# The FFN input by seven block products: constants loaded later, tails stored by fours, another bank for the sums, another order of the steps

## The chip, the cores and the metric

The kernel runs on one core of a Trainium2 chip. Its engines work side by side, each through its own instructions in order: TensorE (PE in the profile; its weight loads are PEld), VectorE (DVE), ScalarE (ACT), GpSimd (POOL) and SyncE (SP, which only issues DMAs). The metric is the device time of one execution in microseconds (us). Lower is better.

## What is computed

One layer of a hybrid decoder for a prompt of 16 meta and 512 ordinary tokens and for 8 samples of 8 tokens, which share all weights. A mixing block (differential attention and a gated delta rule, merged by gates) is followed by an output projection and by a gated feed-forward network (FFN) with a short convolution. The change touches the FFN's input:

```python
xn = rmsnorm(x, p['ln_ffn_pre'])
up, gate = jnp.split(xn @ p['w_ffn_in'], 2, axis=-1)          # 1024 -> 2 x 2816
gate, new_ffn_conv = causal_dwconv(gate, ffn_conv_buf, p['ffn_conv_w'], p['ffn_conv_b'])   # width 3
x = x + rmsnorm((jax.nn.gelu(gate) * up) @ p['w_down'], p['ln_ffn_post'])
```

new_ffn_conv, the last two gate rows of the prompt and of each sample, is an output too; here these rows are called tails. The samples' convolution starts from rows that are given (state_ffn_conv).

## The kernel before

Matrix products are taken in three parts: each operand is split into a high part that TensorE takes exactly (`hi`, a cast on ACT, line 315) and the rest (`lo`, a subtraction on DVE, line 316), and hi x hi, hi x lo and lo x hi are added up (`mm`, line 273).

The stages, in order of time: the input projections; attention, with the paged cache of the samples; the recurrence of the delta rule (`main`) interleaved with a second stream (`rest`), which holds the samples' attention, then `ffn_consts`, then 16 gate products; the mixing; `out_proj`; `ffn_in`; `ffn_out`. `ffn_consts` loads the rows of the convolution's state, weights and bias with 18 small DMAs on ACT's queue, turns them with 22 transposes on PE and copies the result to `fw`, so that each channel's constants lie on its partition.

`ffn_in` works through 22 blocks of 128 channels, block m. The normalised input lies in four pieces of four 128-row slices each: `f["11"]` to `f["22"]`, the first digit for the half of the input channels, the second for the half of the tokens (290 columns). The first three blocks (`PLAIN`) are multiplied plainly (`plain_g` the gate half, `plain_u` the up half), while `differences` forms the sums of pieces t1 to t4 that the other blocks need. From block 3 on, gate and up of a block are one 2 x 2 product of blocks, made from seven products instead of eight, each of 12 matmuls. Per block, in the program's order before:

- `p1`: 11 x f11 into bank A, copied out by ACT (`saved`, line 1745); `p5`: s1 x t1 into bank C, copied out; `p2`: 12 x f21 into a bank "d", whose sum with the copy of p1 is the first half of the gate (`add_g`, lines 1751 to 1757, into `fpre`)
- `weights_g` and `load_u` of the next block: two raw tiles of gate weights (`wraw`, three buffers) and two of up weights (`raw`, three buffers), loaded by SP
- `p6`: s2 x t2 on top of A, copied out as u2; `p4` of the block before, on top of its A: the first up half, which DVE multiplies with the activated gate (`times`, lines 1810 and 1811), then `store`
- `weights_s` of the next block: s1 = a21 + a22 on POOL, s2 = s1 - a11 and s4 = a12 - s2 on DVE (`combine`, line 1711, tiles `sw`, three buffers), each then split (`divide`: `hw` on ACT, `lw` on DVE, seven and six buffers)
- `p3`: s4 x f22 on top of C, whose sum with u2 is the second half of the gate; `conv`: two copies of the tails on POOL (1792, 1793), the first tap on ACT (1797), two more taps on DVE (1799), the GELU on ACT (1802)
- `p7`: s3 x t3 on top of A; DVE adds the copy of p5 (1820), and POOL multiplies with the activated gate (`times` again)
- `weights_r` of the next block: s3 = a11 - a21 on POOL, and the splits of s3 and of a22 ("22"). s3 is the last reader of a21, the split of "22" that of a22; the buffers are then loaded again.

`begin` (line 1763) writes the samples' earlier rows from `fw` into `fpre`, on POOL, at the start of each block. `store` turns a block's 18 tail rows by a transpose into bank "s", copies them by ACT (1833) and sends them with two DMAs from POOL (1835, 1836). The eight banks of PSUM go by tags: two "d", three "t", one "s", and two that serve attention first and are "g" from the recurrence on; A is a "g" here and C a "t". The plain products, and the output projection, take their banks in turn (`psd`).

The text does not set the order of an engine's instructions by itself. A planner lays them out ahead of time: an instruction goes when its inputs and buffers are ready by the planner's own estimate, and among those that are ready the earlier one in the text goes first. Weights are so prepared a block or two ahead, and what the order really was is read from the trace.

## Time and profile before

| | |
|---|---|
| median of 3 runs | 1224.14 us (1222.51 to 1224.27) |
| the profiled execution | 1231.11 us |
| its span, from the first to the last instruction | 1229.4 us |
| mean granted clock of TensorE | 0.975 |
| block loop from block 3 to the last, about | 840 to 1075 us |
| plain blocks, about | 785 to 840 us |
| output projection, about | 740 to 785 us |
| 16 gate products beside the recurrence, from | 529 us |

How to read the lines below: a row of the timeline has the start in the span and the duration in us, the engine, the line of the kernel, the operation, the tile written and those read, the shape and the count; in brackets stands the idle time of the engine ahead of it and what ended that. A row of windows has the stretch, its length, and for each of PE, PEld, DVE, ACT and POOL the busy time with the number of instructions, then the granted clock, the DMA engines' busy share and GB/s. ACTq, POOLq and SPq are the sequencers of these engines, which issue DMAs. In the chain of waits each piece is what the piece after it waited for. The end of a matmul is modelled, and a wait for several things is put down to the one that came last.

### The profile page before, as it was taken

The numbers are of one execution on the slowest core, as the hardware profiler recorded it, in microseconds if no ns is written. First come the engines' busy times: TensorE is split into PE (matmuls) and PEld (weight loads), VectorE is DVE, ScalarE is ACT, GpSimd is POOL, SyncE is SP. The second block draws the span as 40 slices with busy tenths as digits, with TensorE's granted clock in tenths as the row PEclk, the third lists the DMA queues.
The fourth block names the chain that finished last, engine by engine and source line by source line (L and its number), as shares of the span: only waits on it lengthen the run. The fifth ranks groups of instructions, "written<-read, shape, count | busy, mean of one in ns | idle before, by whom it ended". The sixth has DMA issues, their size and how long they took to land. (4 is left out here: it accounts for less than half of the span.)

```text
span 1229.4 us, 23799 instructions
## 1 busy us (share of the span) xinstructions
PE 1151.9 (94%) x8699; PEld 1019.2 (83%) x8699; DVE 741.3 (60%) x1888; ACT 505.5 (41%) x1260; POOL 307.2 (25%) x427
## 2 busy tenths in 40 slices
PE   6999999979989989889999999969999999999996
PEld 5977797757677676589999987869999999999996
DVE  5456667585486487236235754598887878852224
ACT  5244445433343343233234434545554545643322
POOL 2122221141250231112010002473444444400000
PEclk9999999999999999789999999989999999999999
DMA  6274525737836946722322453303333323332222
GB/s 195 76 238 128 158 72 198 231 106 214 300 98 192 313 137 183 230 53 53 86 66 58 129 161 123 112 27 104 87 87 88 88 87 93 124 106 76 86 81 84
DMA packets 185204, 157.57 MB, mean 128 GB/s; under 512 B 13334, under 2 KB 147435, under 8 KB 185087
## 3 DMA queue, kind: packets, MB, share of 16 engines
q1 hardware_dynamic: 179569, 147.53, 39.4%
q0 software_dynamic: 4288, 5.16, 1.5%
q10 hardware_dynamic: 1230, 3.35, 0.9%
q8 instruction: 69, 1.13, 0.4%
q14 instruction: 48, 0.39, 0.1%
HBM read 146.12 MB, written 9.88 MB: 127 GB/s over the span
## 5 line engine op out<-in xcount | busy, mean ns | idle before, releaser
L316 DVE TENSOR_TENSOR wlo<-wraw,whi 128x512 fp32r<-128x512 f32 x196 | 148.6, 775 | 149.5 <-ACT whi L315 147.9
L273 PE MATMUL ps_d<-xhi,whi 128*128 128x256 f32 (+2 forms) x704 | 219.9, 313 | 0.0
L273 PE MATMUL ps_d<-xhi,wlo 128*128 128x256 f32 (+2 forms) x704 | 214.3, 305 | 1.2 <-DVE wlo L316 1.2
L273 PE MATMUL ps_d<-xlo,whi 128*128 128x256 f32 (+2 forms) x704 | 214.3, 304 | 0.3 <-DVE xlo L316 0.2
L315 ACT CAST whi<-wraw 128x512 fp32r<-128x512 f32 x198 | 116.9, 611 | 163.2 <-PE ps_d L273 86.4
L273 PEld LDWEIGHTS ps_d<-xhi,whi 128*128 128x128 f32 x704 | 135.0, 192 | 7.8 <-issue 4.2
L273 PEld LDWEIGHTS ps_d<-xlo,whi 128*128 128x128 f32 x704 | 134.9, 192 | 3.6 <-issue 2.5
L273 PEld LDWEIGHTS ps_d<-xhi,wlo 128*128 128x128 f32 x704 | 134.8, 192 | 2.5 <-DVE wlo L316 1.6
L421 PE MATMUL ps_t<-consts,page 128*128 128x128 f32 x512 | 73.0, 282 | 8.6 <-DVE KT L1405 7.5
L421 PEld LDWEIGHTS ps_t<-consts,page 128*128 128x128 f32 x512 | 57.4, 143 | 25.1 <-issue 10.9
L273 PE MATMUL ps_g<-fhit,hw 128*128 128x290 f32 x228 | 69.6, 305 | 4.5 <-ACT u L1745 3.4
L273 PE MATMUL ps_g<-flot,hw 128*128 128x290 f32 x228 | 68.1, 299 | 0.0
L273 PE MATMUL ps_g<-fhit,lw 128*128 128x290 f32 x228 | 67.8, 297 | 0.0
L1405 ACT COPY KT<-ps_t 128x512 f32<-128x512 f32 x64 | 37.4, 585 | 64.8 <-PE ps_t L421 62.2
L1405 DVE COPY KT<-ps_t 128x512 f32<-128x512 f32 x64 | 43.7, 685 | 18.9 <-PE ps_t L421 18.8
L316 DVE TENSOR_TENSOR lw<-sw,hw 128x512 fp32r<-128x512 f32 x76 | 54.0, 711 | 0.3 <-ACT fy L1802 0.2
L315 ACT CAST hw<-sw 128x512 fp32r<-128x512 f32 x76 | 46.6, 613 | 7.6 <-DVE sw L1711 5.0
L273 PEld LDWEIGHTS ps_g<-fhit,hw 128*128 128x128 f32 x228 | 43.4, 190 | 6.9 <-ACT u L1745 3.9
L1797 ACT ACTIVATE fy<-fpre,fw 128x592 f32<-128x592 f32 x22 | 19.5, 884 | 66.0 <-DVE fpre L1757 66.0
L273 PEld LDWEIGHTS ps_g<-flot,hw 128*128 128x128 f32 x228 | 43.7, 192 | 0.0
L273 PEld LDWEIGHTS ps_g<-fhit,lw 128*128 128x128 f32 x228 | 43.7, 191 | 0.0
L273 PE MATMUL ps_s<-KT,qb 128*32 128x256 f32 x512 | 38.4, 402 | 1.4 <-DVE KT L1405 1.1
(663 smaller groups left out, 3149.3 us busy)
## 6 DMA issues: line engine op xcount, KB each, us to landing
page<-in_cache_k SPq DMA_DIRECT2D x128, 256.0 KB
page<-in_cache_v SPq DMA_DIRECT2D x128, 256.0 KB
wraw<-in_w_in SPq DMA_DIRECT2D x88, 256.0 KB
wraw<-in_w_ffn_in SPq DMA_DIRECT2D x50, 256.0 KB
wraw<-in_w_down SPq DMA_DIRECT2D x40, 256.0 KB
raw<-in_w_ffn_in SPq DMA_DIRECT2D x38, 256.0 KB
wraw<-in_w_out SPq DMA_DIRECT2D x16, 256.0 KB
x<-in_x_prompt SPq DMA_DIRECT2D x4, 512.0 KB
```

The costliest lines, as they stand in the source:

```text
L273: self.nc.tensor.matmul(out, lhsT, rhs, **kw)
L315: self.nc.scalar.copy(hi, raw)
L316: (eng or self.nc.vector).tensor_tensor(out=lo, in0=raw, in1=hi.bitcast(F32), op=ALU.subtract)
L421: self.nc.tensor.transpose(out, in_, self.ident[:k, :k])
L1405: (nc.scalar.copy if j % 2 else nc.vector.tensor_copy)(kt[:, :, 128 * j : 128 * j + 128], tp)
L1797: nc.scalar.activation(y, pre[:, 0:n], AF.Identity, bias=fw[:, m, 19:20], scale=fw[:, m, 16:17])
```

## The change

- `ffn_consts` is no longer called in `rest`. `ffn_in` calls it. It loads wider rows with nine DMAs, into tiles that are later to hold t3 and t4, and that lie where weights of the output projection have lain; the transposes and the copy to `fw` are a function `turn`, called after block 1's first plain gate half.
- Tails are gathered for four blocks in one tile (`TAILS`) and stored together: one transpose, one copy, two DMAs for four blocks, six times in all. The plain blocks call no `store`; the loop calls it after `p4` of the block before, where something waits.
- A is a bank "t" (three), C a bank "g" (two).
- `p7` goes behind `p1` of the next block, and the split of "22" goes behind that `p7`, so `s3` comes directly after `conv` in the text.
- The copy of line 1763 moves from `begin` to `conv`, and some tiles and adds lose their last two columns.

```diff
@@ -240,7 +241,6 @@
                         with ExitStack() as s:
                             yield from self.sample_attention(self.pool(s, "sa", side="right"))
                         self.gates, self.gtpool = {}, self.pool(sm, "gates", side="right")
-                        self.ffn_consts()
                         for i in range(16):
                             yield from self.gate(i)
 
@@ -1657,20 +1657,26 @@
         part(4, r4)
 
 
-    def ffn_consts(self):
+    def ffn_consts(self, pool):
+
         nc, a = self.nc, self.a
-        self.fw = fw = self.t(self.gtpool, [128, NF, 20], "fw", bufs=1)
-        p = self.ps("t")[:, : NF * 20].rearrange("p (k c) -> p k c", k=NF)
-        for k0 in range(0, NF, 4):
-            n = min(4, NF - k0)
-            nat = self.t(self.gtpool, [128, NQ], "gt", bufs=18)[:, : 128 * n]
-            sl = slice(128 * k0, 128 * (k0 + n))
-            nc.scalar.dma_start(nat[:16], a["state_ffn_conv"][0].rearrange("b j c -> (b j) c")[:, sl])
-            nc.scalar.dma_start(nat[16:19], a["ffn_conv_w"][0][:, sl])
-            nc.scalar.dma_start(nat[19:20], a["ffn_conv_b"][:, sl])
-            for k in range(n):
-                self.transpose(p[:, k0 + k], nat[:20, 128 * k : 128 * k + 128])
-        nc.vector.tensor_copy(fw, p)
+        fw = self.t(pool, [128, NF, 20], "fw", bufs=1)
+        rows = []
+        for tag, k0, k1 in (("flot4", 0, 9), ("fhit4", 9, 18), ("flot3", 18, NF)):
+            t = self.t(self.ftpool, [128, 4 * NC], tag)[:, : 128 * (k1 - k0)]
+            sl = slice(128 * k0, 128 * k1)
+            nc.scalar.dma_start(t[:16], a["state_ffn_conv"][0].rearrange("b j c -> (b j) c")[:, sl])
+            nc.scalar.dma_start(t[16:19], a["ffn_conv_w"][0][:, sl])
+            nc.scalar.dma_start(t[19:20], a["ffn_conv_b"][:, sl])
+            rows += [t[:20, 128 * k : 128 * k + 128] for k in range(k1 - k0)]
+
+        def turn():
+            p = self.ps("t")[:, : NF * 20].rearrange("p (k c) -> p k c", k=NF)
+            for k in range(NF):
+                self.transpose(p[:, k], rows[k])
+            nc.vector.tensor_copy(fw, p)
+
+        return fw, turn
 
     def ffn_in(self, sf, gx):
 
@@ -1683,7 +1689,8 @@
             self.t(self.gtpool, [128, NQ], "gt", bufs=18) if m < 18 else None
             for m in range(NF)
         ]
-        fw, f = self.fw, self.f
+        f = self.f
+        fw, turn = self.ffn_consts(pool)
         for j in range(1, 5):
             f[f"t{j}"] = tuple(self.block_t(p, j) for p in ("hi", "lo"))
 
@@ -1729,7 +1736,6 @@
             (a11, a12), (a21, a22) = st["raw"], st["rawu"]
             combine(st, "s3", a11, a21, ALU.subtract)
             divide(st, "s3")
-            divide(st, "22", a22)
 
         def product(ps, wt, x, first):
             hi, lo = wt
@@ -1741,8 +1747,9 @@
                 self.mm(ps, lo[k], xhi[:, k], start=False, stop=k == 3, **kw)
 
         def saved(ps, tag):
-            t = self.t(pool, [128, NC], tag, bufs=2 if tag == "p5" else 1)
-            nc.scalar.copy(t, ps)
+            n = NC if tag == "p1" else NC - 2
+            t = self.t(pool, [128, n], tag, bufs=2 if tag == "p5" else 1)
+            nc.scalar.copy(t, ps[:, :n])
             return t
 
         def add_g(st, half, ps, t):
@@ -1757,14 +1764,11 @@
             nc.vector.tensor_tensor(out=sv[:, 4 * half : 4 * half + 4, 2:10], in0=ss(ps), in1=ss(t), op=ALU.add)
 
         def begin(st):
-            m = st["m"]
-            st["pre"] = pre = self.t(pool, [128, 514 + 80], "fpre", bufs=2)
-            sv = pre[:, 514:].rearrange("p (b j) -> p b j", b=NB)
-            nc.gpsimd.tensor_copy(sv[:, :, 0:2], fw[:, m, 0:16].rearrange("p (b j) -> p b j", b=NB))
+            st["pre"] = self.t(pool, [128, 514 + 80], "fpre", bufs=2)
 
         def p1(st):
             begin(st)
-            st["A"] = self.ps("g")[:, :NC]
+            st["A"] = self.ps("t")[:, :NC]
             product(st["A"], st["11"], f["11"], True)
             st["p1"] = saved(st["A"], "p1")
 
@@ -1777,7 +1781,7 @@
             product(st["C"], st["s4"], f["22"], False)
 
         def p5(st):
-            st["C"] = self.ps("t")[:, :NC]
+            st["C"] = self.ps("g")[:, :NC]
             product(st["C"], st["s1"], f["t1"], True)
             st["p5"] = saved(st["C"], "p5")
 
@@ -1788,19 +1792,24 @@
         def conv(st):
             m, pre = st["m"], st["pre"]
             sv = pre[:, 514:].rearrange("p (b j) -> p b j", b=NB)
-            tail = self.t(pool, [128, 18], "ftail", bufs=2)
+            nc.gpsimd.tensor_copy(sv[:, :, 0:2], fw[:, m, 0:16].rearrange("p (b j) -> p b j", b=NB))
+            i, n = m % TAILS, min(TAILS, NF - m + m % TAILS)
+            if i == 0:
+                self.tails = self.t(pool, [128, 18 * TAILS], "ftail", bufs=1)[:, : 18 * n]
+            tail = self.tails.rearrange("p (r m) -> p r m", m=n)[:, :, i]
             nc.gpsimd.tensor_copy(tail[:, 0:2], pre[:, 512:514])
             nc.gpsimd.tensor_copy(tail[:, 2:18].rearrange("p (b j) -> p b j", b=NB), sv[:, :, 8:10])
-            n = 592
-            y_ = self.t(pool, [128, 594], "fy", bufs=2)
-            y = y_[:, 0:n]
-            nc.scalar.activation(y, pre[:, 0:n], AF.Identity, bias=fw[:, m, 19:20], scale=fw[:, m, 16:17])
+            y_ = self.t(pool, [128, 592], "fy", bufs=2)
+            y = y_
+            nc.scalar.activation(y, pre[:, 0:592], AF.Identity, bias=fw[:, m, 19:20], scale=fw[:, m, 16:17])
             for j in (1, 2):
                 nc.vector.scalar_tensor_tensor(
-                    out=y, in0=pre[:, j : j + n], scalar=fw[:, m, 16 + j : 17 + j], in1=y, op0=ALU.mult, op1=ALU.add
+                    out=y, in0=pre[:, j : j + 592], scalar=fw[:, m, 16 + j : 17 + j], in1=y, op0=ALU.mult, op1=ALU.add
                 )
             nc.scalar.activation(y, y, AF.Gelu_apprx_tanh)
-            st["y"], st["tail"] = y_, tail
+            st["y"] = y_
+            if i == n - 1:
+                waiting.append((m - i, n, self.tails))
 
         def times(eng, st, half, u):
             if gfs[st["m"]] is None:
@@ -1810,30 +1819,36 @@
             eng.tensor_tensor(out=gf[:, sl], in0=y_[:, sl], in1=u[:, 0:256], op=ALU.mult)
             eng.tensor_tensor(
                 out=gf[:, 512 + 32 * half : 544 + 32 * half].rearrange("p (b t) -> p b t", b=4),
-                in0=_strided(y_, 514, 10, TS)[:, 4 * half : 4 * half + 4],
+                in0=y_[:, 512:592].rearrange("p (b j) -> p b j", j=10)[:, 4 * half : 4 * half + 4, 2:10],
                 in1=u[:, 256:288].rearrange("p (b t) -> p b t", b=4),
                 op=ALU.mult,
             )
 
         def p7(st):
             product(st["A"], st["s3"], f["t3"], False)
-            nc.vector.tensor_tensor(out=st["p5"], in0=st["A"], in1=st["p5"], op=ALU.add)
+            nc.vector.tensor_tensor(out=st["p5"], in0=st["A"][:, : NC - 2], in1=st["p5"], op=ALU.add)
             times(nc.gpsimd, st, 1, st["p5"])
 
         def p4(st):
             product(st["A"], st["22"], f["t4"], False)
             times(nc.vector, st, 0, st["A"])
-            store(st)
-
-        def store(st):
-            m = st["m"]
+
+        def store():
+
+            if not waiting:
+                return
+            m, n, tails = waiting.pop()
             tp = self.ps("s")
-            self.transpose(tp[:18, :128], st["tail"])
-            rows = self.t(pool, [18, 128], "ftailT", bufs=1)
-            nc.scalar.copy(rows, tp[:18, :128])
-            sl = slice(128 * m, 128 * m + 128)
-            nc.gpsimd.dma_start(o["new_ffn_conv_prompt"][0, 0, :, sl], rows[0:2])
-            nc.gpsimd.dma_start(o["new_ffn_conv_sample"][0, :, :, sl].rearrange("b j c -> (b j) c"), rows[2:18])
+            self.transpose(tp[: 18 * n, :128], tails)
+            rows = self.t(pool, [18 * TAILS, 128], "ftailT", bufs=1)
+            nc.scalar.copy(rows[: 18 * n], tp[: 18 * n, :128])
+            sl = slice(128 * m, 128 * (m + n))
+            nc.gpsimd.dma_start(
+                o["new_ffn_conv_prompt"][0, 0, :, sl].rearrange("r (m c) -> r m c", c=128), rows[0 : 2 * n]
+            )
+            nc.gpsimd.dma_start(
+                o["new_ffn_conv_sample"][0, :, :, sl].rearrange("b j (m c) -> (b j) m c", c=128), rows[2 * n : 18 * n]
+            )
 
         def plain(ps, w, half, n):
 
@@ -1879,12 +1894,12 @@
         def plain_end(st):
             for half in range(2):
                 times(nc.vector, st, half, st.pop(("u", half)))
-            store(st)
-
-        sts = [{"m": m} for m in range(PLAIN)]
+
+        sts, waiting = [{"m": m} for m in range(PLAIN)], []
         plain_g(sts[0], 0)
         plain_u(sts[0], 0)
         plain_g(sts[1], 0)
+        turn()
         plain_g(sts[0], 1)
         conv(sts[0])
         plain_u(sts[0], 1)
@@ -1911,6 +1926,9 @@
         for m in range(PLAIN, NF):
             st = nxt
             p1(st)
+            if last:
+                p7(last)
+            divide(st, "22", st["rawu"][1])
             p5(st)
             p2(st)
             if m + 1 < NF:
@@ -1919,21 +1937,23 @@
             p6(st)
             if last:
                 p4(last)
+            store()
             if m + 1 < NF:
                 weights_s(nxt)
             p3(st)
             add_g(st, 1, st["C"], st["u2"])
             conv(st)
-            p7(st)
             if m + 1 < NF:
                 weights_r(nxt)
             last = st
+        p7(last)
         self.gf, self.gx, self.ghi, self.glo, self.room = gfs, gx, [], [], []
         for p, j in (("hi", 1), ("lo", 1), ("hi", 2), ("lo", 2)):
             self.make_room(p, j)
         for m in range(7):
             self.divide_gf(m)
         p4(last)
+        store()
 
     def make_room(self, p, j):
```

More of the change, by code (lines that the diff above doesn't have):

```diff
@@ L143 @@
 PLAIN = 3
+TAILS = 4
 FINE = 8
```

## The prediction

> **What bounds the kernel now.** I read the busy table first, then windows by stage, then the chain of waits inside the stage that the change rewrites.
>
> ```profile
> PE 1151.9 (94%) x8699; PEld 1019.2 (83%) x8699; DVE 741.3 (60%) x1888; ACT 505.5 (41%) x1260; POOL 307.2 (25%) x427
> ```
>
> ```profile
> 871.27:1053.41 182.14, 178.27 (x1291) 173.44 (x1290) 149.25 (x287) 94.50 (x196) 90.63 (x136) 1.00 0.31 88
> 1053.41:1064.55 11.14, 11.14 (x84) 10.92 (x83) 8.80 (x18) 7.61 (x17) 4.62 (x9) 1.00 0.25 73
> ```
>
> 94% says that TensorE is nearly full over the whole span, but that is an average. The two windows (length, then busy time of PE, PEld, DVE, ACT, POOL) lie between equal points of the loop over the blocks, the two-column add of line 1755, which runs once a step. The first holds 15 steps: 182.14 / 15 = 12.14 us each. The second holds one step near the end, for which no more weights are prepared: 11.14 us with 84 matmuls (seven products of twelve), and PE never idle. I take 11.2 us as the step that PE alone would set, so these 15 steps lose 15 x 0.94 = 14 us to something else. What it is, the chain shows, here its longest pieces over one step (start, duration, what):
>
> ```profile
> 949.05 1.29 POOL sw L1711
> 950.40 0.57 issue
> 950.98 0.42 DVE fpre L1751
> 951.49 0.61 DVE lw L316
> 952.12 0.69 DVE sw L1711
> 952.82 0.75 DVE fy L1799
> 953.86 0.83 DVE fy L1799
> 954.83 0.50 POOL fpre L1763
> 955.49 0.99 POOL gt L1810
> 956.69 1.28 POOL sw L1711
> 957.99 2.88 DMA raw<-in_w_ffn_in
> 961.03 1.29 POOL sw L1711
> ```
>
> PE isn't in it. It is a ring: the sum s1 on POOL (949.05), s2 on DVE in the "issue" piece, behind it in DVE's queue the second gate half (950.98), one split, s4, and the two convolution taps (952.82, 953.86); then POOL's product with the second up half (955.49), then the difference s3 (956.69), last reader of a raw weight buffer; then the load into that buffer (957.99), and the s1 of a later block waits for that load (961.03). One turn is 961.03 - 949.05 = 11.98 us, and with an odd longer turn the 12.14. DVE and POOL stand in order behind the late s1; PE merely follows.
>
> **The change part by part.**
>
> *Constants out of the gates' stage.* ffn_consts leaves the stream that runs beside the recurrence. ACT's queue there, then PE's, then the window after it:
>
> ```profile
> 522.57 0.33 ACTq L1668 DMA_DIRECT2D gt<-in_state_ffn_conv  x1
> ...
> 528.34 0.26 ACTq L1670 DMA_DIRECT2D gt<-in_ffn_conv_b  x1
> ```
>
> ```profile
> 525.21 1.14 PE L421 MATMUL ps_t<-consts,gt 20*128 20x20 f32 x8
> ...
> 528.90 0.58 PE L421 MATMUL ps_t<-consts,gt 20*128 20x20 f32 x4 [0.52 <-DMA gt<-in_ffn_conv_b]
> 529.42 0.58 PE L273 MATMUL ps_d<-xhi,whi 128*128 128x256 f32 x1
> ```
>
> ```profile
> 540.00:560.00 20.00, 18.60 (x134) 17.23 (x134) 7.97 (x21) 10.66 (x35) 5.78 (x4) 1.00 0.22 54
> ```
>
> From 525.21 to 529.42 PE does these transposes and waits for their rows; a dense gate product follows at once. ACT is held by 18 issues from 522.57 to 528.60. Both go: 529.42 - 525.21 = 4.2 us. What follows is nearly full on PE (18.60 of 20 us), so most of it should stay. Bounds: 0, if the recurrence's own chain sets the stage's end, and 4.5, with the two last transposes that come later. I take **-4.2**, since ACT, which carries that chain too, is released as early.
>
> [...]
>
> *Constants at the end of the output projection.* Nine DMAs on ACT in place of 18: by the rows above (528.34 - 522.57) / 17 = 0.34 us each, 3.1 us of ACT's queue. ACT where their buffers come free:
>
> ```profile
> 779.82 0.46 ACT L412 ACTIVATE y<-y,or 128x192 f32<-128x192 f32 x1 [1.55 <-POOL or L385]
> 781.39 1.06 ACT L1593 ACTIVATE ojunk<-xr 128x1024 bf16<-128x1024 f32 x1 [1.11 <-POOL xr L416]
> ```
>
> ACT idles 2.66 us in front of these two, which hides most; without that cover 3.1 us would fall on the chain that ends the projection. I take **+0.5**. The 22 transposes, 0.14 us each by the row at 525.21, come back on PE just ahead of the stall shown next, at 0 (3 us without it). The copy of fw comes back on DVE, which is full there: **+0.6** for a copy of 440 columns by its neighbours of 0.4 to 0.7 us, up to 1.9 if it is stretched as the split at 828.54 below is.
>
> *The store leaves the plain blocks.* This looks like the largest gain of all. PE's row, two windows, and DVE:
>
> ```profile
> 819.96 0.37 PE L421 MATMUL ps_s<-consts,ftail 128*18 128x128 f32 x1 [10.64 <-POOL ftail L1793]
> ```
>
> ```profile
> 809.30:819.90 10.60, 0.02 (x1) 0.00 (x0) 9.99 (x12) 4.69 (x9) 7.57 (x8) 0.71 0.00 1
> 820.00:824.00 4.00, 4.00 (x18) 4.00 (x19) 3.91 (x7) 3.09 (x6) 2.52 (x3) 0.50 0.25 70
> ```
>
> ```profile
> 819.30 0.42 DVE L1810 TENSOR_TENSOR gt<-fy,ps_s 128x256 f32<-128x256 f32 x1 [0.49 <-ACT fy L1802]
> ...
> 828.54 1.89 DVE L316 TENSOR_TENSOR wlo<-wraw,whi 128x512 fp32r<-128x512 f32 x3
> ```
>
> PE stands for 10.64 us before the first tail's transpose: its bank ps_s still holds an up half, which DVE reads only at 819.30. That transpose goes. But DVE is busy for 9.99 of these 10.60 us, and waits there for ACT, not for PE. Without the stall PE ends block 1 some 10 us sooner and then waits for the low weights that DVE makes at 828.54. So the stall moves to about 820-829, and I take **0**. Bounds: -2.5, DVE's idle share (0.6 in 10.6) over the 45 us of the plain blocks, an estimate; and +2.0, since after the stall PE had clock 0.50 for 4 us, and a new stall that ends later is followed by the same. [...]
>
> *The seven-product loop.* Three edits meet the ring: the copy of line 1763 leaves its place ahead of POOL's product; p7 goes behind the next p1, so that its add (line 1820) is ready later; and s3 is written ahead of that product. DVE and POOL there:
>
> ```profile
> 953.49 0.45 DVE L1820 TENSOR_TENSOR p<-ps_g,p 128x290 f32<-128x290 f32 x1
> ...
> 954.60 0.68 DVE L316 TENSOR_TENSOR lw<-raw,hw 128x512 fp32r<-128x512 f32 x1
> 955.20 0.68 DVE L316 TENSOR_TENSOR lw<-sw,hw 128x512 fp32r<-128x512 f32 x1
> ```
>
> ```profile
> 955.49 0.99 POOL L1810 TENSOR_TENSOR gt<-fy,p 128x256 f32<-128x256 f32 x1 [0.16 <-ACT fy L1802]
> ```
>
> The copy costs the ring nothing: the product also waits for the GELU on ACT, which came 0.16 us later. The add does cost, because it stands between the two taps: 953.86 - 953.49 = 0.37 us. The order on an engine is laid out ahead of time by readiness; with p7 one product later the add should fall behind the second tap, and with a small bubble between dependent taps 0.3 us is won. For s3 its place in the text isn't all: it needs one of three sw buffers, and the one it gets is free when s1's low part has been split, 955.20 + 0.68 = 955.88. The product was ready at 955.49, ahead of that, so POOL most likely still takes it first. Thus 15 x 0.3 = **-4.5**. Bounds: 0 (order as it was) and -14 (ring shorter than PE's step).
>
> The third bank takes away PE's wait for the bank of sums:
>
> ```profile
> 953.26 0.19 PEld L273 LDWEIGHTS ps_g<-fhit,hw 128*128 128x128 f32 x1 [0.36 <-ACT p L1745]
> ...
> 960.25 0.19 PEld L273 LDWEIGHTS ps_g<-fhi,whi 128*128 128x128 f32 x1 [0.41 <-PE ps_g L273]
> ```
>
> These 0.77 us a step are where PE feels the ring. Taken away here they come back elsewhere while the ring is longer than PE's step: 0 by itself; it lets PE take what the ring gives. Of the stores 16 transposes, 16 copies and 32 issues go. They sit on engines with room, and only some six steps outside the 15 are PE's own: **-0.3**. The divide of a22 is put behind p7; it ran behind that add already (954.60): 0.
>
> *Sum:* -4.2 + 0.5 + 0.6 + 0 - 4.5 - 0.3 = -7.9 us. The profiled execution took 1231.1 us (span 1229.4), so its like would take 1223.2. The median of the runs shown, 1224.14, is 7 us lower; the same difference from it gives 1216.
>
> **The rivals.**
>
> (a) *PE-bound.* s3 gets ahead of the product. For it: s3 could have started at 955.88 instead of 956.69, which brings the ring to 11.98 - 0.81 = 11.17, no longer than PE's step, and the text now asks for s3 first. Against it: the product is ready first. The loop gives 14 instead of 4.5: 1216 - 9.5 = **1206.5**.
>
> (b) *The ring stays.* The add keeps its place between the taps. For it: p7 had ended long before its add ran in this trace. Then only the gates' stage pays: -7.9 + 4.5 = -3.4, **1220.7**.
>
> (c) *Slower: the raw buffers.* There are three. a22 is released by the low split of "22" (954.60), which now needs a buffer that p7 frees one product, 11.2 / 7 = 1.6 us, later. In this trace it ends at 955.28, and s3 at 957.97. If it slips by more than those 2.7 us, both loads of the next pair leave after s3, in SP's order, and the one that s1 waits for comes second. Price: between one issue, 0.34 us as on ACT, and one more transfer, 2.88 us; half way 1.6 us a step, 15 x 1.6 = 24 us in place of -4.5: 1216 + 4.5 + 24 = **1245**. Against it: a slip of 1.6 is what to expect.
>
> **How the numbers follow.** Forecast 0.43, (a) 0.28, (b) 0.17, (c) 0.07, and 0.05 for the upper ends together (nothing from the gates, +3.1, +1.9, +2.0). The forecast's own range is 1212 to 1221. To hold 8 in 10 the range takes in (a) with the plain blocks' -2.5, which is 1204, and (b) with part of its upper ends, 1224; outside lie (c), the last case and a little below, 0.17. A measurement of this kernel tells 0.2%, 2.4 us, from no change. Faster than 1221.7: the forecast, (a), and somewhat less than half of (b), 0.76; within: most of the rest of (b), 0.12; slower: 0.12.
>
> **What would show it.** Right: the dense gate product at about 525; DVE as busy as before over 800-845, with PE's stall turned into a wait for wlo; in the loop both taps side by side, the add behind them, and steps of 11.8. Steps of 11.3 with PE idle nowhere show (a), steps of 12.1 with the same chain (b), a load of raw that lands later against s3 (c). The forecast is wrong if POOL or DVE is ordered in the loop in a way that this trace doesn't show, or if the plain blocks aren't DVE's.

## Result and profile after

The changed kernel takes **1216.32 us** (median of 5 runs, 1212.26 to 1217.38) against 1224.27 us before (5 runs, 1222.51 to 1228.41): ratio 0.9924, interval 0.9899 to 0.995, so 6 to 12 us faster. The profiled execution took 1217.38 us (span 1215.6), 13.7 less than the profiled execution of before.

Where the time went is best seen when the same instruction is looked up in the traces of several kernels, and the time from one such landmark to the next is compared. Five of the kernels are experiments of the next section: "consts" is before with the constants' part of the change alone, "tails" with the tails by fours alone, "order" with the order of the steps and the banks alone, "tails+order" is after with the constants in their old place, and "consts+tails" is after with the old order and the old banks. The landmarks are an ACT copy `pT` near 500 us, one of the key norms (ACT `gjunk`, at 540.30 in after and 553.50 in before), a DVE `y` of the output projection's last tiles near 765, the third and the eighteenth low split `lw<-raw` (15 steps of the loop apart; so the row of the plain blocks has the end of the projection and the first steps of the loop in it), an ACT copy `yT` near 1180, and DVE's last `yroot`. Times in us, each a difference of two starts in the timeline of one profiled execution:

```
                     before  tails  order  tails+order  consts  consts+tails  after
gates' stage          53.43  47.37  48.85        49.23   39.72         39.32  39.62
gates to projection  224.72 224.55 222.27       222.41  224.49        223.29 224.71
plain blocks          91.23  91.82  91.39        91.77   90.30         90.56  88.51
15 steps of the loop 182.42 182.17 186.57       184.49  182.06        182.28 180.95
FFN output           145.43 145.56 145.16       145.57  145.47        145.62 145.29
last products         25.20  25.76  25.66        28.14   25.33         25.75  28.53
```

Read the first row first. Wherever the constants are loaded in the gates' stage it takes 47 to 49 us (53 in before's profiled execution), wherever they are not, 39.3 to 39.7. No other row moves by more than 4.2 from before's value. The busy table hardly shows it:

```profile
PE 1143.0 (94%) x8683; PEld 1013.7 (83%) x8683; DVE 748.4 (62%) x1888; ACT 502.8 (41%) x1244; POOL 299.4 (25%) x395
```

94% again. The windows of the stage show it, first of before, then of after (length, busy time of PE, PEld, DVE, ACT, POOL, granted clock, DMA share, GB/s):

```profile
500.00:510.00 10.00, 8.17 (x51) 4.78 (x51) 2.12 (x7) 2.01 (x8) 3.34 (x3) 0.66 0.88 278
...
520.00:530.00 10.00, 6.98 (x47) 5.95 (x44) 3.10 (x13) 2.62 (x11) 1.19 (x2) 0.68 0.37 103
```

```profile
500.00:510.00 10.00, 8.51 (x64) 4.58 (x66) 3.62 (x10) 2.23 (x9) 3.89 (x3) 1.00 0.91 305
...
520.00:530.00 10.00, 10.00 (x76) 9.43 (x74) 2.96 (x10) 2.15 (x6) 1.54 (x2) 1.00 0.03 8
```

The granted clock was 0.68 in the ten microseconds around the constants and is 1.00 now, and PE is busy for all of them. The 0.66 at 500 to 510 is another matter: no other kernel with the constants in that place shows it (1.00 in each), so it belongs to that one execution of before: 53.4 against 48.5, some 5 of the 7 us by which it lay above its median.

The loop, in the chain of waits of after (start, duration, what), one turn:

```profile
932.32 1.30 POOL sw L1718
...
936.10 0.76 DVE fy L1806
...
937.63 0.45 DVE p L1829
938.08 1.20 DVE lw L316 x2
939.28 0.67 POOL gt L1820
939.94 0.02 issue
939.96 1.32 POOL sw L1718
941.27 0.02 issue
941.29 2.96 DMA raw<-in_w_ffn_in
944.25 0.02 issue
944.27 0.04 POOLq L1718
944.32 0.09 issue
944.41 1.29 POOL sw L1718
```

It is the ring of before, with the same members, and a turn of 944.41 - 932.32 = 12.09 us. PE's waits at the start and in the middle of the plain blocks, two rows of PE's timeline:

```profile
785.44 0.40 PE L273 MATMUL ps_t<-fhi,hw 128*128 128x290 f32 x1 [2.01 <-ACT hw L315]
...
811.59 0.58 PE L273 MATMUL ps_s<-fhi,whi 128*128 128x290 f32 x1 [4.60 <-ACT fhit L315]
```

4.60 us in place of 10.64, and 2.01 that are new.

### The profile page after: what moved, and what is told of

Same layout as the page of the kernel before. It is cut to its first block, busy times and chain, and to the rows that moved or that the text cites. A ratio compares the mean times of both kernels' runs of the same rounds, so it can differ in the third digit from the quotient of the medians.

```text
span 1215.6 us, 23653 instructions
## 1 busy us (share of the span) xinstructions
PE 1143.0 (94%) x8683; PEld 1013.7 (83%) x8683; DVE 748.4 (62%) x1888; ACT 502.8 (41%) x1244; POOL 299.4 (25%) x395
## 4 chain that ended last, share of the span: by engine, by line
PE 52%; DVE 17%; issue 15%; DMA 6%; POOL 5%; ACT 3%; SPq 0%; ACTq 0%; DVEq 0%; POOLq 0%
PE ps_d L273 22%; PE ps_g L273 9%; PE ps_t L273 8%; PE ps_s L273 6%; PE ps_t L421 6%; DMA raw<-in_w_ffn_in 2%; POOL sw L1718 2%; DVE lw L316 2%; DVE cy L651 1%; DMA page<-in_cache_v 1%; PE ps_m L273 1%; DVE KT L1405 1%; DVE fy L1806 1%; DVE gt L316 1%; DVE sw L1718 1%
## 5 line engine op out<-in xcount | busy, mean ns | idle before, releaser
L273 PE MATMUL ps_t<-fhit,hw 128*128 128x290 f32 x228 | 70.7, 310 | 3.7 <-DVE p L1829 3.1
L273 PE MATMUL ps_t<-flot,hw 128*128 128x290 f32 x228 | 67.6, 296 | 0.0
L273 PE MATMUL ps_t<-fhit,lw 128*128 128x290 f32 x228 | 67.5, 296 | 0.0
L316 DVE TENSOR_TENSOR lw<-sw,hw 128x512 fp32r<-128x512 f32 x76 | 62.4, 821 | 0.3 <-ACT hw L315 0.2
L273 PEld LDWEIGHTS ps_t<-fhit,hw 128*128 128x128 f32 x228 | 42.9, 188 | 9.4 <-DVE p L1829 6.4
L273 PEld LDWEIGHTS ps_t<-flot,hw 128*128 128x128 f32 x228 | 43.3, 190 | 0.0
L273 PEld LDWEIGHTS ps_t<-fhit,lw 128*128 128x128 f32 x228 | 43.1, 189 | 0.0
```

The costliest lines, as they stand in the source:

```text
L273: self.nc.tensor.matmul(out, lhsT, rhs, **kw)
L316: (eng or self.nc.vector).tensor_tensor(out=lo, in0=raw, in1=hi.bitcast(F32), op=ALU.subtract)
```

## The experiments

### One part of the change at a time

**The constants alone.** `ffn_consts` and `turn` as in the change, the copy of the samples' earlier rows moved to `conv`, the rest as before.

```diff
-                        self.ffn_consts()
...
-        fw, f = self.fw, self.f
+        f = self.f
+        fw, turn = self.ffn_consts(pool)
...
         plain_g(sts[1], 0)
+        turn()
```

> Before, with the constants' part of the change alone (nine loads at the end of the output projection, the turn after block 1's first plain gate half, the copy of the samples' earlier rows moved to conv). Theory 1, most of the gain is the gates' stage (4.2 us of PE) less what the end of the projection gives back: 3 to 6 us faster than before, so 1218 to 1221, with the first dense gate product at about 519 to 525 us in place of 529. Theory 2, the gain comes from the loop and the order of its steps: within 2 us of before. In both the 10.64 us wait of PE ahead of the first tail's transpose is still there.

Measured: 1215.12 us, ratio 0.9914 (0.9897 to 0.9932). That is 11 us, more than either theory gave it, and no less than the whole change. The wait ahead of the first tail's transpose, in PE's timeline, is still there and 1.9 us shorter:

```profile
812.15 0.37 PE L420 MATMUL ps_s<-consts,ftail 128*18 128x128 f32 x1 [8.73 <-DVE gt L1817]
```

**The tails alone.** `store` by fours, called once a step, none in the plain blocks; `saved` and `p7`'s add two columns narrower for room.

```diff
             times(nc.vector, st, 0, st["A"])
-            store(st)
...
                 p4(last)
+            store()
```

> Before, with the storing of tails by fours alone (and the narrower copies that make room for it). Theory 1: the 10.64 us wait of PE in the plain blocks goes, a shorter one comes later, and 1 to 4 us are won over the plain blocks, so 1220 to 1223; the loop keeps its 12.1 us a step. The prediction's own term says 0 here and 0.3 for the stores that are gone. Theory 2: within 1 us of before.

Measured: 1227.52 us, ratio 1.0008 (0.9999 to 1.0017): nothing that can be told, as in theory 2. PE's rows show what became of the 10.64 us:

```profile
815.38 0.58 PE L274 MATMUL ps_s<-fhi,whi 128*128 128x290 f32 x1 [6.16 <-DVE gt L1818]
...
824.65 0.61 PE L274 MATMUL ps_s<-fhi,wlo 128*128 128x290 f32 x1 [4.95 <-DVE wlo L317]
```

6.16 + 4.95 = 11.11 us of waits, the second of them for `wlo` where the prediction had put it. Taking away one of PE's waits moved it and did not shorten it.

**Order and banks alone.**

```diff
-            st["A"] = self.ps("g")[:, :NC]
+            st["A"] = self.ps("t")[:, :NC]
...
-            st["C"] = self.ps("t")[:, :NC]
+            st["C"] = self.ps("g")[:, :NC]
...
             p1(st)
+            if last:
+                p7(last)
+            divide(st, "22", st["rawu"][1])
             p5(st)
...
             conv(st)
-            p7(st)
```

> Before, with the order of the steps and the banks alone: A is a bank t and C a bank g, p7 stands behind the next block's p1, and the split of 22 behind that p7. Theory 1, the ring still sets the step: 12.1 us a step and a time within 1.5 us of before. Theory 2, and the prediction's own term: the add of line 1820 falls behind both taps and the step is 11.8 us, 4 to 5 us faster than before.

Measured: 1230.78 us, ratio 1.004 (1.0027 to 1.0052): 5 us slower, against both theories. The loss is in the loop (186.57 in the table). Two loads of its chain of waits:

```profile
929.98 3.09 DMA raw<-in_w_ffn_in
...
942.15 4.04 DMA raw<-in_w_ffn_in
```

The work between is the same in each step; some loads last 1 us longer.

**All but the constants**, that is after with the constants in their old place.

> After, with the constants loaded in the gates' stage as before (so tails by fours, the order of the steps and the banks are there). Theory 1: 1 to 4 us faster than before and 3 to 6 us slower than after, so 1220 to 1223; PE has the transposes at about 525 us again. If the granted clock is again below 0.8 at 500 to 530 us, that dip belongs to the constants' place there; if it is 1.00, the dip was that one execution's. Theory 2: nearly all of the 8 us stay, 1217.

Measured: 1230.64 us, ratio 1.0042 (1.0028 to 1.0055): 14 us slower than after, beyond both theories. The clock from 520 to 530 is 0.54. It is low (0.54 to 0.68) in before, tails, order and tails+order, and 1.00 in after, in consts alone and in consts with tails. The dip belongs to the constants' place.

**Constants and tails**, that is after with the old order and the old banks.

> After, with the old order of the steps and the old banks (so the constants' part and the tails by fours alone). Theory 1, order and banks are worth nothing by themselves because the ring sets the loop: within 2 us of after, 1214 to 1218, 12.1 us a step. Theory 2, they win here the 2 us that after's trace has in the loop over that of the constants alone: 1218 to 1219. Theory 3, they cost what they cost with the constants in the old place (5 us): 1211 to 1213.

Measured: 1214.76 us, ratio 0.9906 (0.9891 to 0.9921). After's interval and this one overlap: order and banks win nothing that can be told. Theory 1 holds.

### What in the gates' stage costs

Constants in their old place, the 18 DMAs too, but the transposes, now a function that `ffn_consts` returns, behind the third gate product.

```diff
-                        self.ffn_consts()
+                        turn = self.ffn_consts()
                         for i in range(16):
                             yield from self.gate(i)
+                            if i == 2:
+                                turn()
```

> Before, with the constants' 18 DMAs issued on ACT where they were, but their 22 transposes placed after the third gate product instead of ahead of the first. Theory 1, what the constants cost in the gates' stage is PE standing for their rows and the low clock (0.5 to 0.7 at 520 to 530 us) that follows: PE starts the dense product at about 519 us at clock 1.00, and 5 to 9 us are won, 1217 to 1221. Theory 2, it is ACT, held by 18 issues from about 517 to 523 us, that delays the recurrence and the products' copies: the first dense product may start early, but the stage ends no sooner and the time is within 2 us of before, 1224 to 1228.

Measured: 1229.64 us, ratio 1.0019 (1.0007 to 1.0032). Nothing is won; it is 2 us slower. Its timeline, ACT first and then PE, and its window:

```profile
516.58 0.27 ACT L901 COPY gv<-ps_g 128x128 f32<-128x128 f32 x1 [0.41 <-PE ps_g L275]
516.74 0.33 ACTq L1670 DMA_DIRECT2D gt<-in_state_ffn_conv  x1
...
523.61 0.26 ACTq L1672 DMA_DIRECT2D gt<-in_ffn_conv_b  x1
523.92 0.75 ACT L1504 ACTIVATE gt<-ps_d 128x256 f32<-128x256 f32 x2 [7.07 <-DMA gt<-in_ffn_conv_w]
...
524.36 0.58 PE L275 MATMUL ps_d<-xhi,whi 128*128 128x256 f32 x1 [5.22 <-ACT gt L1504]
```

```profile
516.00:518.00 2.00, 0.94 (x6) 0.78 (x7) 0.62 (x5) 0.43 (x3) 0.58 (x1) 1.00 0.69 191
518.00:520.00 2.00, 0.97 (x7) 0.63 (x5) 0.63 (x5) 0.00 (x0) 0.61 (x1) 0.85 0.92 243
520.00:522.00 2.00, 0.00 (x0) 0.00 (x0) 0.00 (x0) 0.00 (x0) 0.00 (x0) 0.50 0.25 66
...
526.00:528.00 2.00, 2.00 (x12) 2.00 (x11) 1.26 (x6) 0.27 (x1) 0.71 (x1) 0.50 0.00 0
528.00:530.00 2.00, 2.00 (x12) 2.00 (x12) 0.42 (x2) 0.00 (x0) 0.00 (x0) 0.59 0.00 0
```

No transpose stands in front of the dense product now, and it starts no sooner. PE idles 5.22 us for ACT's copy out of a bank "d", and that copy stands in ACT's queue behind the 18 issues: the last of them ends at 523.61 + 0.26 = 523.87, the copy starts at 523.92. (Issues don't count as busy, so the row calls the 7.07 us idle and names a DMA.) In after the same copy stands directly behind the same `gv`, from ACT's timeline:

```profile
517.38 0.27 ACT L899 COPY gv<-ps_g 128x128 f32<-128x128 f32 x1 [0.41 <-PE ps_g L273]
517.55 0.72 ACT L1502 ACTIVATE gt<-ps_d 128x256 f32<-128x256 f32 x2
```

PE's clock falls to 0.50 at about 519.4 (0.85 is the mean of the slice) and stays there until about 529.6, for 5 us of dense work. Theory 2 holds in its cause, ACT. But the dense product, which that theory let start early, didn't, and the time is 1.6 us above its range.

Then the same with the 18 DMAs issued by SP in place of ACT (`nc.scalar` to `nc.sync` in three lines), and nothing else changed.

> As the kernel with the transposes after the third gate product, but the 18 DMAs are issued by SP, not by ACT; nothing else differs. Theory, formed after that run: what costs is ACT's queue, in which 18 issues (516.74 to 523.87 us) stand ahead of the copies that free the banks of the first dense products; PE idles 5.2 us for them and then runs at clock 0.5 until about 529. Then ACT is free at about 517 here, the dense products start at about 519 at clock 1.00, and 6 to 9 us are won against before: 1218 to 1221. If the loads' mere presence, their landing or the transposes cost it, the time stays at 1226 to 1230. If SP's weight loads now stand behind the 18 issues, PE waits for weights a little later and part of the gain is lost, 1221 to 1225.

Measured: 1232.86 us, ratio 1.0056 (1.004 to 1.0072), 3 to 5 us slower still: the theory's number failed. In its timeline:

```profile
533.21 0.69 ACT L1504 ACTIVATE gt<-ps_d 128x256 f32<-128x256 f32 x2
...
534.51 0.56 PE L275 MATMUL ps_d<-xhi,whi 128*128 128x256 f32 x1
```

ACT was free, but the order laid out for it now has the recurrence's activations first and this copy at 533.21, 9 us later than with ACT issuing. So the edit did not do what it was to do. It speaks for the copy all the same. The start of ACT's copy and of the dense product in the kernels so far:

```
                         ACT's copy   dense product
before                       528.65          529.42
tails                        524.96          525.59
order                        525.00          525.76
tails+order                  523.68          524.53
transposes later             523.92          524.36
the same, DMAs on SP         533.21          534.51
consts                       517.14          518.67
consts+tails                 515.86          517.40
after                        517.55          519.08
```

The product follows the copy by 0.4 to 1.5 us in all nine, with the transposes in front of it or not. In the last three it doesn't wait for the copy: it follows the recurrence's matmuls.

### What sets the loop

If the ring of the raw loads sets the step, something that opens it must shorten the step. In after, s3 needs one of the three sw buffers. The first edit writes s3 over a11, which has no later reader.

```diff
-            combine(st, "s3", a11, a21, ALU.subtract)
+            nc.gpsimd.tensor_tensor(out=a11, in0=a11, in1=a21, op=ALU.subtract)
+            st["rs3"] = a11
```

> After, with s3 = a11 - a21 written over a11, so that it needs none of the three sw buffers and needn't wait for the split of s1's low part. Theory 1, the ring (load of raw, s1, s2, split of s1, s3, load of raw) sets the step and this wait is part of it: s3 starts 2 to 4 us earlier after s1, the loads of raw land before POOL asks for them, and the step falls from 12.1 to between 11.2 and 11.6 us, 8 to 14 us faster than after: 1202 to 1208. Theory 2, DVE's order or another buffer sets the step: 12 us still, within 2 us of after. Theory 3: a11's buffer comes free later and the wraw loads take over, slower than after.

Measured: 1217.59 us, ratio 0.9933 (0.9919 to 0.9946), the same as after. The edit did act. In the timeline (DVE, then POOL's s1, s3 and next s1, then SP's two loads of raw) s3 starts 2.4 us after s1 began, where it was 7.6:

```profile
940.90 0.68 DVE L316 TENSOR_TENSOR lw<-raw,hw 128x512 fp32r<-128x512 f32 x1
...
932.54 1.57 POOL L1718 TENSOR_TENSOR sw<-raw,raw 128x512 f32<-128x512 f32 x1 [1.63 <-DMA raw<-in_w_ffn_in]
934.97 1.28 POOL L1737 TENSOR_TENSOR wraw<-wraw,raw 128x512 f32<-128x512 f32 x1 [0.86 <-DVE sw L1718]
...
944.78 1.41 POOL L1718 TENSOR_TENSOR sw<-raw,raw 128x512 f32<-128x512 f32 x1 [1.79 <-DMA raw<-in_w_ffn_in]
...
936.28 0.37 SPq L1710 DMA_DIRECT2D raw<-in_w_ffn_in  x1
...
941.67 0.37 SPq L1710 DMA_DIRECT2D raw<-in_w_ffn_in  x1
```

But s1 needs both raw buffers. The load into the second leaves at 941.67, right behind the low split of "22" on DVE (940.90), s1 still waits 1.79 us for it, and a turn is 944.78 - 932.54 = 12.24 us. The ring closes over the other raw buffer. In the chain of waits most pieces are PE's now, with ACT's copy of p1 between them, for which PE waits about 0.5 us a step; whether that or the second buffer sets the 12.1 us that are left, this run doesn't tell.

The same edit on the constants' part alone, with the old order and banks:

> Before with the constants' part alone, and s3 written over a11. Theory 1, as with the edit on after: 8 to 14 us faster than 1215 (1201 to 1207) if the ring alone sets the step whatever the order of the steps; if the changed order and the third bank are what lets PE take a shorter ring, this one gains clearly less than the edit on after, 3 to 6 us. Theory 2: within 2 us of 1215.

Measured: 1222.42 us, ratio 0.9963 (0.995 to 0.9977), 6 to 7 us slower than without the edit, and against both theories. The loss isn't in the loop, of which 15 steps take 182.15 us (182.06 without the edit): by the landmarks of the first table it is in the row of the plain blocks, 95.75 against 90.30.

A fourth sw buffer, paid for with an lw buffer:

```diff
-            t = self.t(w7, [128, 4, 128], "sw", bufs=3)
+            t = self.t(w7, [128, 4, 128], "sw", bufs=4)
...
-            hi, lo = (self.t(w7, [128, 4, 128], tag, F32R, bufs=n) for tag, n in (("hw", 7), ("lw", 6)))
+            hi, lo = (self.t(w7, [128, 4, 128], tag, F32R, bufs=n) for tag, n in (("hw", 7), ("lw", 5)))
```

> After, with a fourth sw buffer, and one lw buffer fewer to make room. Theory 1: s3 no longer waits for the split of s1's low part, as with s3 in place; the step falls below 11.8 us, 4 to 14 us faster than after, unless the fifth lw buffer is missed. Theory 2: the wait for the buffer was not what held s3, within 2 us of after or slower by the missing lw buffer.

Measured: 1221.18 us, ratio 0.9961 (0.9946 to 0.9975), 5 us slower than after. s3 does start sooner, 5.8 us after s1 in the mean of the same 15 steps in place of 7.6, and these take 187.21 us all the same. The run can't say which of the two buffers did it.

Both raw buffers at once: s3 over a11 and s4 over a12, two sw buffers, and the memory of the third as a fourth raw buffer.

```diff
-            combine(st, "s4", a12, st["rs2"], ALU.subtract, nc.vector)
+            nc.vector.tensor_tensor(out=a12, in0=a12, in1=st["rs2"], op=ALU.subtract)
+            st["rs4"] = a12
...
-                t = self.t(w7, [128, 4, 128], "raw", bufs=3)
+                t = self.t(w7, [128, 4, 128], "raw", bufs=4)
```

> After, with a fourth raw buffer in the memory of the third sw buffer, which isn't needed when s3 is written over a11 and s4 over a12. Theory 1, the ring through the raw loads sets the step (in after the buffer that s3 releases, with s3 in place the one that the low split of 22 releases at 8.76 us of a 12.1 us step): with a fourth buffer both loads land before POOL asks for them, and the step is what PE needs, 11.3 us, plus its waits for banks of 0.2 to 0.6: 6 to 12 us faster than after, 1204 to 1210. Theory 2, the order on DVE and ACT (the tap behind s2 and s4, p1's copy behind the tap) sets 12.1 us whatever the buffers: within 3 us of after. Theory 3: the wraw buffers, now held until the splits of s3 and s4, take over, slower than after.

Measured: 1235.57 us, ratio 1.0079 (1.006 to 1.0097), 19 us slower than after: theory 3. Two rows of its waits from 870 to 1040 us, some 13 steps (total us, times, longest):

```profile
ACT whi L315 <- DMA wraw<-in_w_ffn_in: 23.1, 13, 2.2
...
PEld ps_t L273 <- DVE p L1831: 21.4, 14, 1.9
```

No wait for a raw load is left among them. The gate weights' load has taken its place, since their buffers are now held until the splits of s3 and s4 are done, and PE waits for the add behind it. With the old order and banks:

> The constants' part and the tails by fours with the old order and the old banks, and the fourth raw buffer. Theory 1: as with the edit on after, if the ring is all that lies above PE's step: 1204 to 1210. If the third bank and the place of p7 are what lets PE take a shorter ring, PE waits for the bank g of A here (with s3 in place it waited 1.2 us a step) and this is 4 us or more slower than the same edit on after. Theory 2: within 3 us of 1215.

Measured: 1223.72 us, ratio 0.9981 (0.9969 to 0.9993), 9 us slower than without the edit: theory 3 of the run before, on the old order too.

Three ways to open the ring, in five kernels, left no step shorter than after's. Behind each wait that was taken away stood another of nearly the same length: the second raw buffer, the bank g (1.2 us a step with s3 in place and the old banks), the gate weights' buffers. That the raw ring is the longest of them was argued from the chain; that it is the only one is refuted.

## Why the prediction was right, and where it was wrong

The time was right, 1216 against 1216.3, but that it came so near is luck: the terms were wrong in opposite directions. The gates' stage gave 4.7 us more than forecast and the plain blocks 2.7, the costs of 1.1 did not show; the loop gave 3.2 less, and the last products, in no term, cost 2.9. As the level of the kernels with the constants in the old place I take the mean of tails, order and tails+order, 48.5 us for the gates' stage, since before's own profiled execution had the low clock at 500.

**Gates' stage, -4.2: right in sign, half the size.** Measured 39.62 - 48.5 = -8.9, and the dense product at 519, not 525. The step that failed is "Both go: 529.42 - 525.21 = 4.2 us". It counts the time from the first transpose to the dense product. But PE's idle time began earlier, with ACT's copy, which the 18 issues held. From the landmark near 500 us the dense product starts 24.5 us later in the three kernels (23.95, 24.34, 25.10) and 18.4 later in after: 6.1 us. The rest, 2.8, is mostly the clock: by the clock's record in each trace it was 0.50 for 2.8, 5.4 and 4.6 us of dense work in the three, so half of that was lost, 1.4 to 2.7 us, and after doesn't have it at all; some 0.2 to 0.3 are the two late transposes. That the transposes weren't the cause is shown by the run that moved them; that ACT's copy is, rests on the row that names it, on its place in ACT's queue and on the nine kernels, as the run with SP did not isolate it. The text had named ACT, and then took its release for no more than PE's share.

The clock is in no term of the forecast for this stage, and it was part of the gain. In after the first dense matmuls follow the recurrence's without a gap (519.08), and the clock stays at 1.00. In the clock's record the low stretch is 6.83 us long in tails, 10.24 in order, tails+order and the run with the later transposes, 13.65 with the DMAs on SP: two, three and four times 3.41, the length of the shortest in before. PE was not idle throughout ahead of the fall: in the run with the later transposes it was busy for 0.94 of the 2 us from 516 to 518, and in tails its longest gap from 515 to 522 was 1.22 us.

**Constants at the projection's end, +0.5, and the copy of fw, +0.6: no cost left over.** PE does wait 2.01 us for ACT at 785.44 in after, and ACT's `fpre` copy 3.43 us behind the issues. With the constants alone, though, the later stall is 8.73 us in place of 10.64, and the plain blocks are 0.9 us shorter: PE's 2 us came out of PE's own waiting. The nine issues took 3.8 us of ACT's queue (780.41 to 784.22), the copy of `fw` 0.60 us of DVE, as forecast, and the 22 transposes 1.5 us of PE, not 3. The bound of 1.9 for the copy rested on a misreading: the row at 828.54 holds three splits (x3) of 0.68 us, not one that was stretched.

**The store in the plain blocks, 0: right by itself, not in the whole change.** Tails alone moved the 10.64 us to 11.11, the second part waiting for `wlo`. The whole change wins 2.7 us over this stage (88.51 against 91.23), just beyond the bound of 2.5, and the wait for `wlo` that was to show it isn't there: of the long waits only the 4.60 us for ACT's `fhit` are left. Consts with tails has 90.56, so 2 of them come only with the order and the banks. Why, no run tells.

**The loop, -4.5: nearest to rival (b), though not by its reason.** The ring stays, but not because the add kept its place. The steps are of 12.1 us, not 11.8 or (a)'s 11.3, and (c)'s second raw buffer came to count only when s3 was written in place. 15 steps take 1.3 us less (180.95 against the mean of 182.30 of before and tails). The add did fall behind both taps, as the prediction put it, and POOL's product did start sooner: 938.52 - 932.32 = 6.20 us after s1, where it was 955.49 - 949.05 = 6.44. But s3 starts at 939.96 - 932.32 = 7.64, and that is 956.69 - 949.05 = 7.64 too. The step that failed is "0.3 us is won": it priced POOL's product as it stood in before. The timeline of after, POOL and then DVE:

```profile
938.52 0.75 POOL L1819 TENSOR_TENSOR gt<-fy,p 128x256 f32<-128x256 f32 x1 [2.96 <-ACT fy L1809]
939.23 0.70 POOL L1820 TENSOR_TENSOR gt<-fy,p 128x32 f32<-128x32 f32 x1
...
938.00 0.68 DVE L316 TENSOR_TENSOR lw<-raw,hw 128x512 fp32r<-128x512 f32 x1
938.60 1.23 DVE L316 TENSOR_TENSOR lw<-sw,hw 128x512 fp32r<-128x512 f32 x1
```

The small product takes 0.70 us, where it took 0.25 before, and the split beside it 1.23, where the one before it took 0.68. The split ends at 938.60 + 1.23 = 939.83, the small product 0.10 us later. Before, the large product was the one that took longer, 0.99 us beside the split at 955.20, and POOL's small product ran while DVE stood idle (POOL's row, then DVE's):

```profile
956.44 0.25 POOL L1811 TENSOR_TENSOR gt<-fy,p 128x32 f32<-128x32 f32 x1
...
956.20 0.18 DVE L1757 TENSOR_TENSOR fpre<-ps_d,p 128x32 f32<-128x32 f32 x1
956.77 1.74 DVE L316 TENSOR_TENSOR wlo<-wraw,whi 128x512 fp32r<-128x512 f32 x1 [0.39 <-ACT whi L315]
```

So the 0.24 us that were won at the taps were lost beside DVE's splits (0.70 us for 0.25, 1.23 for 0.68). Why the two take longer side by side, these rows don't show.

That this holds for every variant that leaves the buffers as they were is seen when the ring is cut in two, from the start of s1 to the end of s3 and from there to the next s1, as means over the same 15 steps of each timeline, those after the first two:

```
               s1 to the end of s3   to the next s1   (lowest to highest)
before                 8.91               3.25            3.03 to 3.66
tails                  8.91               3.24            3.09 to 3.32
consts                 8.91               3.23            3.11 to 3.31
consts+tails           8.91               3.24            2.99 to 3.35
order                  8.89               3.55            3.05 to 4.32
tails+order            8.94               3.36            3.07 to 4.49
after                  8.94               3.12            2.97 to 3.32
```

The new order leaves the first part as it was, within 0.03 us. What differs is the second, the load. 15 x 0.3 = 4.5 us of it make up the 4.3 that order loses in the loop, and 15 x 0.12 = 1.8 most of the 2.2 of tails+order. The 1.3 us that after wins lie there too (15 x 0.12 = 1.8), not at the taps, where the term had them. Why the load takes up to 4 us in the two kernels with the new order and the constants in the old place, and not in after, stays open.

**The last products, not in the prediction: +2.9.** In after's chain PE waits there for one load, and the 63 matmuls behind it are slow; the chain, then the window:

```profile
1178.98 4.95 DMA wraw<-in_w_down
...
1185.33 10.79 PE ps_d L273 x63
```

```profile
1185.00:1190.00 5.00, 5.00 (x25) 5.00 (x26) 2.96 (x7) 2.79 (x13) 0.00 (x0) 0.66 0.09 26
```

The same two pieces of consts+tails:

```profile
1179.59 3.71 DMA wraw<-in_w_down
...
1184.71 9.25 PE ps_d L273 x63
```

The load is 1.2 us longer, and the low clock that follows costs 1.5 more. It is the loss of the gates' stage once more, a gap and a clock of 0.50 behind it, by the record from 1185.93 to 1189.35. tails+order shows both (28.14; 4.61 and 10.76). The three variants of the changed kernel in the section on the loop have the long load (4.48 in the one with s3 in place) without the low clock, 26.5 to 27.0 for the row. The kernels that lack the tails by fours or the new order have 25.2 to 25.9. So a part of the 2.9, about 1, goes with tails and order together, and the low clock came in two of five executions; why the load is longer, no run tells.

The sum of what was measured, each term against the level named with it, -8.9 - 2.7 - 1.3 + 2.9 = -10.0, is near the 10.4 between the profiled executions of tails and after (1227.79 and 1217.38). One more sentence was wrong without harm: "the same difference from it gives 1216". Of before's 7 us above its median some 5 were its low clock at 500, which no other execution shows, and after's profiled execution lies 1.1 us above its own median. By that the forecast of 1223.2 for a profiled execution was 5.8 us too high, and the median came out right.

No run beats the changed kernel by more than can be told: the constants alone (0.9914) and with tails (0.9906) have intervals that overlap with its own. The constants are the change; the rest is worth nothing that these runs show.

## What to carry to other kernels

In the run with the later transposes 18 small DMAs, issued by ACT between its computations, held the copy behind them in its queue from 516.74 to 523.87 us, and PE for 5.22: look for the copy that frees a PSUM bank there, and count both PE's gap and the low clock behind it (0.50 for 5 us of dense work). When an edit takes a wait from a ring, price the neighbours that will then run at the same time, and look for the second buffer over which the ring closes. Before the offset of one profiled execution from the median is carried over, look where in the trace it lies.

## What the runs showed of the hardware that was not expected

- In the run with the later transposes 18 issues on ACT took from 516.74 to 523.87 us, 0.25 to 0.33 us each with gaps between, and beside and behind them PE's clock was 0.50 for 10.24 us, 5 of them dense work (2.8 to 5.4 in tails, order and tails+order).
- By the clock's record of before and after every stretch at 0.50, but for the one at the end of each, is 3.41, 6.83, 10.24 or 13.65 us long: 9 of them in before, 7 in after. In the 3.41 us ahead of 17 of the 18 falls PE was busy for 52% or less; ahead of the other, at 503.11 in before, for 76%. The ends of matmuls are modelled, so the shares are estimates. PE's longest gap just ahead of the fall at 523.59 in before was 1.01 us.
- A load of 256 KB in the loop took 2.88 to 4.04 us in the chains shown, with the same loads around it; a mean of 0.3 us more a step made up the 4.3 us that order alone lost in the loop.
- POOL's multiplication of 32 columns took 0.25 us with DVE idle (before, 956.44) and 0.70 beside a split (after, 939.23), DVE's split of 512 columns 0.68 with POOL idle for most of it (after, 938.00) and 1.23 beside POOL's two products (after, 938.60).
